# A two-layer decoder on one core: the RWKV-7 recurrence taken 16 heads at a time instead of 8

## The chip, the cores and the metric

One core of a Trainium2 chip. A core has a matrix engine (TensorE, PE in the profile, with its weight loads as PEld), VectorE (DVE), ScalarE (ACT), GpSimd (POOL) and SyncE (SP, which issues the DMAs here). The metric is the device time of one execution in microseconds; a kernel is described by the median of its runs.

## The reference, cut to what matters

The model has two layers on 272 tokens (16 meta tokens and 256 others) of width 2048, each a token mixer and a squared-ReLU MLP. The mixer of layer 0 is RWKV-7 with 32 heads of 64; that of layer 1 is gated linear attention and is not touched here. The part around the change is this:

```python
def step(S, inp):
    r_t, w_t, k_t, v_t, a_t, b_t = inp
    sa = jnp.einsum('bhvk,bhk->bhv', S, a_t)
    S = S * w_t[:, :, None, :] + sa[..., None] * b_t[:, :, None, :] + v_t[..., None] * k_t[:, :, None, :]
    y = jnp.einsum('bhvk,bhk->bhv', S, r_t)
    return S, y
_, y = lax.scan(step, S0, xs)
...
mu = jnp.mean(y, axis=-1, keepdims=True)
var = jnp.mean(jnp.square(y - mu), axis=-1, keepdims=True)
y = ((y - mu) * lax.rsqrt(var + RW_GN_EPS)).reshape(B, T, D) * ln_w + ln_b
out = ((y + bonus).astype(x.dtype) * g) @ w_o
```

Every head carries a 64x64 state S through all tokens. The kernel does not step by token: it takes chunks of 64 tokens (four of them and a last one of 16). Inside a chunk the dependence of a token on earlier ones is a triangular system, which is inverted; from chunk to chunk only S is passed.

## The kernel before, in words

All activations lie transposed: a tile of 128 features by 272 tokens, 16 such tiles (f = 0 to 15), each with two heads. Weights come as blocks of 128x1024 in float32; `wload` (L126) has one DMA into `raw` (3 buffers), ScalarE rounds to `hi` and VectorE takes the rest as `lo` (2 buffers each), and `mm3` (L140) makes a product of three matmuls of 272 columns.

The mixer has three stretches that matter.

**The k loop** (L468 to L517). For each f it makes the key projection (48 matmuls), reads the decay and the learning rate back from HBM, and writes two tiles, `bk` and `ar`, to HBM (L491, L494). Two small matmuls hang on it, at L481 and L496; the second needs `kn` from VectorE. At f = 3 the first group's tiles are read back by `load(0)` (L417); from f = 5 to 9 `scores` makes the group's products of keys and queries, one chunk a time; from f = 10 the inversion of group 0 runs, 9 steps in each f.

**The products.** The v projection (256 units), then the output projection (256 units) are cut into units of three matmuls. `R(n)` runs n units, `until(n)` runs units up to the n-th; they fill TensorE between the steps of the recurrence. Units 0 to 255 are v; the output projection follows, and what it needs is `split` from the normed tiles of four f each: units 256, 288, 384 and 448 are the first that need the next four.

**The recurrence** (L784 to L857). TensorE's order is written out by hand there (`manual_schedule`); the order of the other engines is the scheduler's, which takes program order as priority and puts weight loads ahead of the rest. Four groups of 8 heads are taken one after the other, and each goes through five chunks:

- `scores` (L423) makes a chunk's products; two VectorE multiplies with a mask write them into `AM`.
- `invert` (L439) is VectorE's: 8 transposes into `sysA` (2 more for the last chunk), 30 steps of two tensor ops each, 12 transposes back. It is written as a generator, and `some(inv, n)` puts n steps at a place in the order. `merge` (L539) then joins two inverted blocks of 32 into one of 64, by two rounds of 32x32 matmuls with ScalarE copies between.
- `centre` (L569) takes the values, for two chunks at once, `keys` (L582) transposes the keys.
- `inner`, `state`, `sides`, `solve`, `carry`, `learn`, `emit` (L590 to L657) are the chunk itself: `state` applies S from the last chunk, `sides` copies the right side negated, `solve` applies the inverse, `learn` makes the new S (ScalarE scales it in four pieces, L647), `emit` the output. Each works through its heads by small matmuls whose even and odd heads lie in different halves of the array.
- `norm` (L659) is the group norm and the gate of four f; it follows each group.

A chunk's step waits for the step before it, so units stand between: `GAPS` (L46) has their number ahead of `solve` and ahead of `learn`, for each group and chunk. `MARK` (L51) has the unit up to which units run before a group's inversion must be done.

In the order of TensorE, the scores of group g+1 lie in chunks 0 and 1 of group g, its inversion runs from there to `until(MARK[g])`, and then `merge(g+1)` follows:

```python
until(MARK[g])
some(inv, 99)
m = merge(g + 1)
next(m)
```

Of the kernel before, what the change touches and what calls it, by code (L numbers as in the profile page):

```python
# [1 line left out]

# [15 lines left out]
P = 128  # L18
# [27 lines left out]
GAPS = [[(4, 3), (4, 3), (8, 7), (8, 7), (6, 6)],  # L46
# [3 lines left out]

MARK = [162, 256, 366]  # L51
# [5 lines left out]
class Kern:  # L57
# [210 lines left out]
    def rwkv(self, done):  # L268
# [147 lines left out]
        def fetch(g, dst, src, a=0, b=576):  # L416
            nc.sync.dma_start(dst[g % 2][:, :, a:b], src[4 * g : 4 * g + 4, :, a:b].rearrange("f p n -> p f n"))  # L417

        def load(g):
            fetch(g, BKs, bkd)  # L420
            fetch(g, ARs, ard)

        def scores(g, c):  # L423
            BK, AR, AM, AMr = (b[g % 2] for b in (BKs, ARs, AMs, AMrs))
            n = C if c < NC4 else 32
            cs = slice(c * 128, c * 128 + 2 * n)

            pv = [self.ptr().rearrange("p (h m) -> p h m", h=4)[: 2 * n, :, : 2 * n] for _ in range(2)]
            for p in range(4):
                for q in range(2):  # L430
                    rows = slice(64 * q, 64 * q + 64)
                    nc.tensor.matmul(pv[q][:, p], BK[rows, p, cs], AR[rows, p, cs], start=True, stop=True)  # L432
            dst, mk = (AM[:, c], self.maskA) if c < NC4 else (AMr, self.maskR)
            for q in range(2):
                tt(dst[:, q::2], pv[q], mk.unsqueeze(1).to_broadcast([2 * n, 4, 2 * n]))
# [3 lines left out]
        def invert(g):  # L439
            AM, AMr = AMs[g % 2], AMrs[g % 2]  # L440
            X = sysA
            diag = lambda u: AM[64 + 32 * u : 96 + 32 * u, :, :, 32 * u : 32 * u + 32].rearrange("p c h t -> p t c h")
            part = [slice(8 * k, 8 * k + 8) for k in range(4)]
            nc.gpsimd.memset(X[64:96], 0.0)
# [4 lines left out]
            for k in part[:2]:  # L449
                nc.vector.transpose(X[96:128, k], AMr[32:64, :, k].rearrange("p h t -> p t h").unsqueeze(2)  # L450
                                    .to_broadcast([32, 8, 4, 8]))
                yield
            nc.gpsimd.memset(X.rearrange("p a b -> p (a b)")[:, ::33], 1.0)
            for s in range(1, 31):
                n, m = 31 - s, s
                w = self.t(lp, [P, 256], "upd", 1)[:, : n * m].rearrange("p (a b) -> p a b", a=n)
                tt(w, X[:, s + 1 :, s : s + 1].to_broadcast([P, n, m]), X[:, s : s + 1, :m].to_broadcast([P, n, m]))
                tt(X[:, s + 1 :, :m], X[:, s + 1 :, :m], w, ALU.add)
                yield
# [8 lines left out]
        for f in range(KT):  # L468
# [30 lines left out]
            if f == 0:  # L499
# [4 lines left out]
                BKs, ARs = ([self.t(lp, [P, 4, 576], n)] for n in ("BK0", "AR0"))  # L504
                AMs, AMrs = [self.t(lp, [P, NC4, 8, 128], "AM0")], [self.t(lp, [64, 8, 64], "AMr0")]
                sysA = self.t(lp, [P, 32, 32], "sysA")
                t11 = sysA.rearrange("p a b -> p (a b)")[64:96].rearrange("p (c h s) -> p c h s", c=NC4, h=8)
# [14 lines left out]
        BKs.append(self.t(kp, [P, 4, 576], "BK1"))  # L522
        ARs.append(self.t(kp, [P, 4, 576], "AR1"))
        AMs.append(self.t(kp, [P, NC4, 8, 128], "AM1"))
        AMrs.append(self.t(kp, [64, 8, 64], "AMr1"))
        sb = self.t(kp, [P, 4, HEAD], "S")
        half = lambda x: x[:, :256].rearrange("p (h v) -> p h v", h=4)
        uvs, ras, bkts, rys, pSs = {}, {}, {}, {}, {}

        def geom(g, c):  # L530
            full = c < NC4
            n = C if full else 32
            lo, up = slice(0, n), slice(n, 2 * n)


            return full, n, C if full else T - NC4 * C, (AMs[g % 2][:, c] if full else AMrs[g % 2]), lo, up, (up, lo)


        def merge(g):  # L539
            AM, AMr = AMs[g % 2], AMrs[g % 2]  # L540
            rg = self.t(kp, [P, 512], "rs", 2)[32:64].rearrange("p (t s) -> p t s", t=16)
            nc.vector.transpose(rg, sysA[96:128, 0:16])
            nc.vector.tensor_copy(AMr[32:64, :, 0:16].rearrange("p h t -> p t h"), rg[:, :, 0:8])
            qs = {}
            for c in (0, 2):

                pq = self.ptr()
                qs[c] = self.t(kp, [P, 512], "rs", 2) if c else self.t(kp, [P, 4, P], "bkt", 1).rearrange("p a b -> p (a b)")
                for h in range(8):
                    for i in range(2):  # L550
                        nc.tensor.matmul(pq[64 + 32 * i : 96 + 32 * i, 32 * h : 32 * h + 32], AM[64:96, c + i, h, 32:64],
                                         t11[:, c + i, h], start=True, stop=True)
                for i in range(2):
                    nc.scalar.copy(qs[c][96:128, 256 * i : 256 * i + 256], pq[64 + 32 * i : 96 + 32 * i, :256])
            yield
            for c in (0, 2):
# [557 lines left out]
```

## Time and profile before

| what | value |
|---|---|
| median of 3 runs | 2589.22 us (2586.8 to 2591.66) |
| the profiled execution | 2593.35 us |
| its span | 2591.6 us |
| PE busy | 2543.9 us (98%) |
| DVE busy | 1664.5 us (64%) |
| ACT busy | 1262.3 us (49%) |
| PE busy, 296 to 671 us of the span | 351.10 of 375.00 us |
| DVE busy there | 280.67 us |
| ACT busy there | 200.83 us |

The stretch from 296 to 671 us holds the units and the recurrence; the k loop lies ahead of it. A busy PE is not PE at its peak: matmuls are pipelined, and a record lasts longer than the time to the next one's start. In the timeline, the distance of starts is what a matmul costs. One float32 matmul of the recurrence stands as two records, while one of the units (rounded operands) stands as one. PEclk is the share of TensorE's clock that was granted.

### The profile page before, as it was taken

The numbers are of one execution on the slowest core, as the hardware profiler recorded it, in microseconds if no ns is written. First come the engines' busy times: TensorE is split into PE (matmuls) and PEld (weight loads), VectorE is DVE, ScalarE is ACT, GpSimd is POOL, SyncE is SP. The second block draws the span as 40 slices with busy tenths as digits, with TensorE's granted clock in tenths as the row PEclk, the third lists the DMA queues.
The fourth block names the chain that finished last, engine by engine and source line by source line (L and its number), as shares of the span: only waits on it lengthen the run. The fifth ranks groups of instructions, "written<-read, shape, count | busy, mean of one in ns | idle before, by whom it ended". The sixth has DMA issues, their size and how long they took to land.

```text
span 2591.6 us, 47101 instructions
## 1 busy us (share of the span) xinstructions
PE 2543.9 (98%) x19222; PEld 2351.8 (91%) x19222; DVE 1664.5 (64%) x2749; ACT 1262.3 (49%) x2055; POOL 11.4 (0%) x36
## 2 busy tenths in 40 slices
PE   9999999999999999999999999999999999999998
PEld 8898888888999999999999988998888888888887
DVE  8677977885655545445456676668666656656565
ACT  5475555546544334334334455445555435445444
POOL 0000000000000000000000000000000000000000
PEclk9999999999999999999999999999999999999999
DMA  5476733432455555545555544444555555555554
GB/s 202 169 246 236 231 133 112 133 112 98 163 176 174 179 174 177 179 172 179 176 174 179 173 153 147 147 154 171 187 188 188 189 189 189 187 187 187 188 189 160
DMA packets 137082, 450.14 MB, mean 174 GB/s; under 512 B 15760, under 2 KB 23696, under 8 KB 136864
## 3 DMA queue, kind: packets, MB, share of 16 engines
q1 hardware_dynamic: 136864, 447.12, 50.0%
q8 instruction: 151, 2.47, 0.4%
q14 instruction: 67, 0.55, 0.1%
HBM read 431.07 MB, written 15.99 MB: 173 GB/s over the span
## 4 chain that ended last, share of the span: by engine, by line
PE 89%; DVE 7%; ACT 1%; issue 1%; DMA 1%; DVEq 0%; POOL 0%; ACTq 0%; SPq 0%; POOLq 0%
PE pj L170 24%; PE pj L142 14%; PE pj L144 14%; PE pj L143 14%; PE pj L171 12%; DVE lo L137 2%; DVE sysA L270 1%; DVE upd L270 1%; PE pj L197 1%; PE pt L432 1%; PE pm L684 1%; DVE AM L465 1%; DVE sysA L447 1%; PE pt L949 1%; ACT hi L136 0%
## 5 line engine op out<-in xcount | busy, mean ns | idle before, releaser
L136 ACT CAST hi<-raw 128x1024 fp32r<-128x1024 f32 (+2 forms) x838 | 814.0, 979 | 1105.4 <-PE pj L143 589.6
L137 DVE TENSOR_TENSOR lo<-raw,hi 128x1024 fp32r<-128x1024 f32 (+2 forms) x838 | 946.5, 1136 | 576.0 <-ACT hi L136 567.8
L142 PE MATMUL pj<-x,hi 128*128 128x272 f32 x2272 | 674.1, 297 | 9.9 <-DVE hres L270 6.4
L144 PE MATMUL pj<-x,lo 128*128 128x272 f32 x2272 | 659.5, 290 | 6.4 <-DVE lo L137 6.2
L143 PE MATMUL pj<-x,hi 128*128 128x272 f32 x2272 | 658.6, 290 | 0.6 <-DVE x L270 0.6
L170 PE MATMUL pj<-x,hi 128*128 128x512 f32 x1664 | 585.8, 396 | 0.6 <-DVE x L868 0.6
L171 PE MATMUL pj<-x,lo 128*128 128x256 f32 x1664 | 466.7, 281 | 1.3 <-DVE lo L137 1.3
L142 PEld LDWEIGHTS pj<-x,hi 128*128 128x128 f32 x2272 | 430.6, 190 | 18.9 <-issue 6.3
L144 PEld LDWEIGHTS pj<-x,lo 128*128 128x128 f32 x2272 | 430.3, 189 | 9.3 <-DVE lo L137 8.2
L143 PEld LDWEIGHTS pj<-x,hi 128*128 128x128 f32 x2272 | 433.3, 191 | 3.3 <-DVE x L270 0.9
L170 PEld LDWEIGHTS pj<-x,hi 128*128 128x128 f32 x1664 | 312.5, 188 | 77.0 <-issue 2.9
L170 PE MATMUL pj<-h,hi 128*128 128x512 f32 x1024 | 358.5, 394 | 0.0
L171 PEld LDWEIGHTS pj<-x,lo 128*128 128x128 f32 x1664 | 313.3, 188 | 2.2 <-DVE lo L137 1.9
L142 PE MATMUL pj<-h,hi 128*128 128x272 f32 x1024 | 294.7, 288 | 0.0
L144 PE MATMUL pj<-h,lo 128*128 128x272 f32 x1024 | 293.9, 287 | 0.0
L143 PE MATMUL pj<-h,hi 128*128 128x272 f32 x1024 | 293.5, 287 | 0.0
L171 PE MATMUL pj<-h,lo 128*128 128x256 f32 x1024 | 288.5, 282 | 0.0
L170 PEld LDWEIGHTS pj<-h,hi 128*128 128x128 f32 x1024 | 192.4, 188 | 44.5
L143 PEld LDWEIGHTS pj<-h,hi 128*128 128x128 f32 x1024 | 193.7, 189 | 0.0
L171 PEld LDWEIGHTS pj<-h,lo 128*128 128x128 f32 x1024 | 193.5, 189 | 0.0
L142 PEld LDWEIGHTS pj<-h,hi 128*128 128x128 f32 x1024 | 192.6, 188 | 0.0
L144 PEld LDWEIGHTS pj<-h,lo 128*128 128x128 f32 x1024 | 192.1, 188 | 0.0
(247 smaller groups left out, 2104.5 us busy)
## 6 DMA issues: line engine op xcount, KB each, us to landing
raw<-mlp_w_d SPq DMA_DIRECT2D x512, 512.0 KB, 3.3
raw<-gla_in_d SPq DMA_DIRECT2D x98, 512.0 KB, 3.2
raw<-w_rkv_d SPq DMA_DIRECT2D x80, 512.0 KB, 3.6
raw<-gla_o_d SPq DMA_DIRECT2D x32, 512.0 KB, 3.2
raw<-rw_oQ_d SPq DMA_DIRECT2D x24, 512.0 KB, 3.3
raw<-w_r_d SPq DMA_DIRECT2D x16, 512.0 KB, 3.3
ard<-ar SPq DMA_DIRECT2D x16, 288.0 KB, 4.0
bkd<-bk SPq DMA_DIRECT2D x16, 288.0 KB, 4.0
```

Of the source, the lines that this page charges most:

```text
L136: nc.scalar.copy(hi[:, h], raw[:, h])
L137: nc.vector.tensor_tensor(out=lo[:, h], in0=raw[:, h], in1=hi[:, h].bitcast(F32), op=ALU.subtract)
L142: nc.tensor.matmul(out, hi[:, ws], xh, start=first, stop=False)
L143: nc.tensor.matmul(out, hi[:, ws], xl, start=False, stop=False)
L144: nc.tensor.matmul(out, lo[:, ws], xh, start=False, stop=last)
L170: nc.tensor.matmul(wide, hi[:, ws], x[kt][:, :, off : off + SEQ], start=kt == 0, stop=False)
L171: nc.tensor.matmul(ps[:, :SEQ], lo[:, ws], x[kt][:, 0, off : off + SEQ], start=False, stop=kt == nk - 1)
L197: nc.tensor.matmul(ps[:, :n], raw[:, j * P : (j + 1) * P], x(kt), start=kt == 0, stop=kt == 8 * len(srcs) - 1)
L270: tt = lambda o, a, b, op=ALU.mult: nc.vector.tensor_tensor(out=o, in0=a, in1=b, op=op)
L432: nc.tensor.matmul(pv[q][:, p], BK[rows, p, cs], AR[rows, p, cs], start=True, stop=True)
L447: nc.vector.transpose(X[32 * u : 32 * u + 32, k], diag(u)[:, k])
L465: nc.vector.transpose(diag(u)[:, k], X[32 * u : 32 * u + 32, k])
```

## The change

Two halves of 16 heads take the place of four groups of 8. A half's four chunks and the last one are inverted in two blocks: block 2g has chunks 0 and 1, block 2g+1 has chunks 2, 3 and the last. `scores`, `invert` and `merge` go by these blocks, and `b` or `c > 1` picks the buffer.

- In the k loop, `load(0)` comes at f = 7 and reads 256 columns of eight f; the scores of block 0 come at f = 10 to 13; the inversion starts after f = 13, 6 steps in each f.
- The products start with 10 units, then five times 16 units and a piece of block 1's scores, with 7 steps of inversion 0 each. Merge 0 comes at unit 120.
- `MARK` = 120, 176, 244, 326 are the units ahead of merges 0, 1, 2 and 3; merges 1 and 3 lie between chunks 1 and 2. The gaps are 4 or 5 units.
- The scores of block 2 lie in chunks 2 and 3 of the first half, and its inversion runs from chunk 3. The scores of block 3 come after the first `inner` of the second half.
- The norms of the first eight f lie before and around merge 2, those of the other eight at the end.
- `centre` takes one chunk of 16 heads: two matmuls side by side, each with 64 tokens. `solve` makes the even heads first, copies them, then the odd heads. `state` sets its products for the right side ahead of most of those for the output. `learn` scales S by one VectorE multiply instead of four ScalarE ops.
- A block that holds chunks 0 and 1 is inverted on 64 partitions, the other on 128; the ops have the same free size as before.

The core of the diff:

```diff
-GAPS = [[(4, 3), (4, 3), (8, 7), (8, 7), (6, 6)],
-        [(4, 3), (4, 3), (8, 7), (8, 7), (6, 6)],
-        [(3, 2), (3, 2), (8, 7), (8, 7), (6, 6)],
-        [(4, 4), (4, 4), (4, 4), (4, 4), (4, 4)]]
-MARK = [162, 256, 366]
+GAPS = [[(4, 4), (4, 4), (5, 4), (5, 4), (5, 5)],
+        [(4, 4), (4, 4), (5, 4), (5, 4), (5, 5)]]
+MARK = [120, 176, 244, 326]
...
-            if f == 3:
+            if f == 7:
                 load(0)
-            if 4 < f < 10:
-                scores(0, f - 5)
-            if f == 9:
+            if 9 < f < 14:
+                scores((f - 10) // 2, f % 2)
+            if f == 13:
                 inv = invert(0)
-            if f > 9:
-                for _ in range(9):
+            if f > 13:
+                for _ in range(6):
                     next(inv, None)
...
 def centre(g, c):
-            for p in range(4):
-                nc.tensor.matmul(pv[:w, p * P : (p + 1) * P], hres[:, 4 * g + p, c * C : c * C + w], self.cent,
-                                 start=True, stop=True)
+            for p in range(4):
+                for e in range(2):
+                    nc.tensor.matmul(pv[64 * e : 64 * e + nr, p * P : (p + 1) * P], hres[:, 8 * g + 4 * e + p, c * C : c * C + nr],
+                                     self.cent, start=True, stop=True)
...
 def state(g, c):
-            turns = [(p, q, i) for p in range(4) for q, i in ((0, 0), (1, 1), (1, 0), (0, 1))]
-            if not full:
-                turns.sort(key=lambda x: x[2])
+            pq = [(p, q) for p in range(8) for q in range(2)]
+            turns = [(*x, 0) for x in pq]
+            outs = [(p, 1 - q, 1) for p, q in pq]
+            if full:
+                for i in range(7):
+                    turns.insert(1 + 3 * i, outs.pop(0))
+            for p, q, i in turns + outs:
...
 def solve(g, c):
-            for h in range(8):
-                o = n * (1 - h % 2)
-                nc.tensor.matmul(pu[o : o + nu, h // 2], am[up, h, :nu], rs[up, h], start=True, stop=True)
             for q in range(2):
                 o = n * (1 - q)
+                for h in range(q, 16, 2):
+                    nc.tensor.matmul(pu[o : o + nu, h // 2], am[up, h, :nu], rs[up, h], start=True, stop=True)
                 nc.scalar.copy(uv[n : n + nu, q::2], pu[o : o + nu])
...
 def learn(g, c):
-            for p in range(4):
-                nc.scalar.mul(sb[:, p], pS[:, p], WC[:, 4 * g + p, c : c + 1])
+            tt(sb, pS, WC[:, 8 * g : 8 * g + 8, c : c + 1].to_broadcast([P, 8, HEAD]))
...
         load(1)
         ahead()
         with tc.manual_schedule(engines={mybir.EngineType.PE}):
-            until(52)
-            m = merge(0)
+            R(10)
+            for c, e in ((2, 0), (2, 1), (3, 0), (3, 1), (4, 0)):
+                some(inv, 7)
+                R(16)
+                scores(c, e)
+            for g in range(2):
+                last, quarter = nothing, 0
+                if g:
+                    last = norm(0)
+                    some(last, 1)
+                    for _ in range(4):
+                        R(3)
+                        some(last, 2)
+                    last = chain(last, norm(1))
+                until(MARK[2 * g])
+                some(inv, 99)
+                m = merge(2 * g)
+                next(m)
...
+                until(128 + 128 * g)
+                centre(g, 0)
...
+                inv = invert(2 * g + 1)
                 for c in range(5):
+                    if c == 2:
+                        until(MARK[2 * g + 1])
+                        some(inv, 99)
+                        m = merge(2 * g + 1)
...
                     if c:
                         state(g, c)
+                    if g == 0 and c in (2, 3):
+                        scores(c - 2, 0)
                     R(GAPS[g][c][0])
-                    some(inv, 9)
+                    some(inv, 11)
                     solve(g, c)
-                    if c in (1, 3):
+                    if c < 4:
                         centre(g, c + 1)
+                    if g == 0 and c in (2, 3):
+                        scores(c - 2, 1)
                     if c < 4:
                         carry(g, c)
                     R(GAPS[g][c][1])
+                    if g == 0 and c == 3:
+                        inv = invert(2)
+                    some(inv, 11)
...
+                    if g == 0 and c == 1:
+                        load(2)
+                    if g == 0 and c == 4:
+                        load(3)
+            for g in (2, 3):
+                for _ in norm(g):
+                    R(g)
```

More of the change, by code (lines that the diff above doesn't have):

```diff
@@ L1 @@
 from contextlib import ExitStack
+from itertools import chain
 import numpy as np
@@ L430, in scores, with load @@
+        def load(b):
+            fetch(b, BKs, bkd)
+            fetch(b, ARs, ard)
+        def scores(c, e):
+            BK, AR = BKs[c > 1], ARs[c > 1]
+            n, np = (C, 4) if c < NC4 else (32, 8)
+            o = 128 * (c % 2) if c < NC4 else 256
+            cs = slice(o, o + 2 * n)
+            pv = [self.ptr().rearrange("p (h m) -> p h m", h=np)[: 2 * n, :, : 2 * n] for _ in range(2)]
+            for p in range(np):
                 for q in range(2):
                     rows = slice(64 * q, 64 * q + 64)
-                    nc.tensor.matmul(pv[q][:, p], BK[rows, p, cs], AR[rows, p, cs], start=True, stop=True)
@@ L590, in inner @@
         def inner(g, c):
-            full, n, nr, am, lo, up, at = geom(g, c)
+            full, n, nr, am, lo, up, at = geom(c)
             uv = uvs[g, c]
-            ra = ras[g, c] = half(self.pu())
-            for h in range(8):
-                nc.tensor.matmul(ra[at[h % 2], h // 2], am[:n, h, :n], uv[:n, h], start=h < 2, stop=c == 0 and h > 5)
+            ra = ras[g, c] = bank(self.pu())
+            for h in range(16):
+                nc.tensor.matmul(ra[at[h % 2], h // 2], am[:n, h, :n], uv[:n, h], start=h < 2, stop=c == 0 and h > 13)
@@ L606, in state @@
         def state(g, c):
[L607 to L614 removed]
+            full, n, nr, am, lo, up, at = geom(c)
+            AR, ra = ARs[c > 1], ras[g, c]
+            o = 128 * (c % 2) if full else 256
```

237 lines of the change are left out of this document (101 added, 136 removed).

## The prediction

> **What bounds the kernel now.** I read the page first, then windows, the timeline of PE, the waits of PE and the groups of VectorE.
>
> ```profile
> span 2591.6 us, 47101 instructions
> PE 2543.9 (98%) x19222; PEld 2351.8 (91%) x19222; DVE 1664.5 (64%) x2749; ACT 1262.3 (49%) x2055; POOL 11.4 (0%) x36
> ```
>
> TensorE sets the end: a gain must take matmul time away or close holes in PE. The change touches the k loop and the recurrence, so I asked for windows: 210 to 230 us in the k loop, three that reach from the first to the last VectorE op of an inversion, and one between inversions. Behind the window stand its length and the busy time of PE, PEld, DVE, ACT and POOL, then PEclk.
>
> ```profile
> 210.00:230.00 20.00, 17.28 (x116) 15.70 (x115) 8.71 (x19) 7.09 (x14) 0.00 (x0) 0.74 0.64 239
> 350.85:396.45 45.60, 42.19 (x547) 38.09 (x545) 43.20 (x105) 21.78 (x55) 0.69 (x2) 1.00 0.38 135
> 432.85:478.75 45.90, 43.65 (x578) 40.06 (x579) 43.45 (x104) 22.98 (x58) 0.69 (x2) 0.96 0.37 134
> 510.15:561.95 51.80, 46.75 (x587) 43.24 (x586) 49.80 (x121) 23.52 (x55) 0.68 (x2) 1.00 0.27 94
> 400.00:432.00 32.00, 30.95 (x448) 27.04 (x446) 15.81 (x29) 20.00 (x47) 0.94 (x1) 1.00 0.35 110
> ```
>
> While an inversion runs, DVE is busy for 43.2 of 45.6 us, 95%, and PE idles for 3.4, 2.2 and 5.1 us, 10.7 in all. Between inversions DVE is half free. So the recurrence is bound by PE, with holes where VectorE is short. The second window, asked for the inversion's tile alone:
>
> ```profile
> 350.85:396.45 45.60, 0.00 (x0) 0.00 (x0) 33.22 (x83) 0.17 (x1) 1.00 0.38 135
> ```
>
> An inversion is 33.2 us of VectorE, and there are four of them before and after.
>
> **Small matmuls: minus 9.2 us.**
>
> ```profile
> 343.26 0.27 PE L620 MATMUL pu<-S,AR 64*64 64x64 f32 x1
> 343.27 0.27 PE L617 MATMUL pry<-AR,S 64*64 64x64 f32 x1
> 343.28 0.27 PE L620 MATMUL pu<-S,AR 64*64 64x64 f32 x1
> ...
> 343.37 0.22 PE L620 MATMUL pu<-S,AR 64*64 64x64 f32 x1
> ...
> 343.72 0.22 PE L620 MATMUL pu<-S,AR 64*64 64x64 f32 x1
> ...
> 343.89 1.16 PE L432 MATMUL pt<-AR,BK 64*128 64x128 f32 x16
> 344.98 0.39 PE L142 MATMUL pj<-x,hi 128*128 128x272 f32 x1
> 345.21 0.29 PE L143 MATMUL pj<-x,hi 128*128 128x272 f32 x1
> 345.33 0.29 PE L144 MATMUL pj<-x,lo 128*128 128x272 f32 x1
> ```
>
> `state` of 8 heads is 16 matmuls in 8 rounds of four records each. Rounds lie 0.058 us apart (343.37 to 343.72, six steps), yet the group takes from 343.26 to 343.89, 0.63 us: 0.16 beyond eight rounds, paid where a group begins and ends. Unit matmuls lie 0.125 apart, so a unit is 0.375 us; the first distance of a run is 0.23, and with its end I take 0.2 more for a run. Groups of double length halve their number: inner, solve and emit fall from 20 to 10 each, learn, state and keys from 16 to 8, and 54 x 0.16 is 8.6 us. The runs of units hardly change (71 to 67).
>
> ```profile
> 347.29 1.16 PE L574 MATMUL pm<-cst,hres 128*128 128x128 f32 x8
> 348.38 1.16 PE L432 MATMUL pt<-AR,BK 64*128 64x128 f32 x16
> 349.47 0.70 PE L639 MATMUL pu<-S,cst 128*128 128x256 f32 x2
> 349.82 0.48 PE L142 MATMUL pj<-x,hi 128*128 128x272 f32 x1
> ```
>
> `centre` took 1.09 us, twelve times (four of them for the last chunk). With two column halves side by side, its 16 records should take what the 16 paired ones of L432 take, 1.09, ten times: minus 2.2, of which I take 1.6. `carry`, 0.35 us, at most doubles and halves its number: 0. `state` gives up its rounds of four: 16 products for the right side need 16 rounds, as many as two groups had, and the outputs that find no partner cost up to ten rounds more, 0.6 us, six times; I take 1, between 0 and 3.5.
>
> `solve` is the open price. Its even and odd heads alternated between two column halves; now eight matmuls of one half stand ahead of eight of the other. Paired they cost 16 rounds, one behind another 32: 0.93 us more, ten times, 9.3. In the rows above each matmul stands as two records, and L617's first record starts ahead of L620's second: a matmul does pass earlier ones that use another quarter, three of them in a round of four. I take 0, since eight is not far from three, and keep 9.3 as the other end.
>
> The Trainium skill ("TensorE: Matmul & The Clock Gate", Part 3: Packing small matmuls) says that matmuls start and end strictly in program order. By it the sum would be 9.3 us higher. The alternating rows do not agree with it.
>
> **The k loop: minus 10.6 us.** Its timeline on PE, and two waits of PE from 170 to 320 us:
>
> ```profile
> 205.09 0.73 PE L481 MATMUL pm<-sq,cst 128*128 128x272 f32 x2
> ...
> 212.28 0.72 PE L481 MATMUL pm<-sq,cst 128*128 128x272 f32 x2
> 215.72 2.08 PE L432 MATMUL pt<-AR,BK 64*128 64x128 f32 x16 [2.72 <-DMA AR<-ard]
> ...
> 218.13 0.43 PE L143 MATMUL pj<-x,hi 128*128 128x272 f32 x1
> 218.35 0.43 PE L144 MATMUL pj<-x,lo 128*128 128x272 f32 x1
> ```
>
> ```profile
> PE pu L496 <- DVE kn L492: 3.4, 4, 1.4
> PE pt L551 <- DVE sysA L461: 1.5, 1, 1.5
> ```
>
> The first scores wait 2.7 us for the read-back of `AR`, and then a matmul takes 0.22 us instead of 0.125. PEclk is 0.74 over these 20 us: 5.2 us of clock are missing, so some 10.4 us ran at half; the slowdown from 0.125 to 0.22 loses 0.43 of that, 4.5 us. An f takes 7.2 us (205.09 to 212.28). With the load at f = 7 and the scores at f = 10, three f lie between where two lay, so `AR` comes 4 us early instead of 3 us late: minus 2.7 and 4.5. The inversion took 33 us of VectorE out of f = 10 to 15; 12 of its 52 steps stay, so I let 2.8 of the 3.4 us at L496 go. One small piece of scores (0.6 us) leaves the loop. Bounds: 0, if VectorE and the read-back stay late, to minus 13, if every delay of those f goes.
>
> **VectorE's windows: plus 13.3 us.**
>
> ```profile
> L137 DVE TENSOR_TENSOR lo<-raw,hi 128x512 fp32r<-128x512 f32 x100 | 64.4, 686 | 12.3 <-ACT hi L136 11.6
> L270 DVE TENSOR_TENSOR AM<-pt,cst 128x512 f32<-128x512 f32 x24 | 15.5, 686 | 23.5 <-PE pt L432 23.5
> L270 DVE TENSOR_TENSOR hres<-pj,hres 128x272 f32<-128x272 f32 x22 | 9.6, 438 | 23.9 <-PE pj L144 23.1 <-DMA hres<-hT_d 0.8
> L679 DVE SCALAR_TENSOR_TENSOR ysq<-hres,vecs,ysq 128x272 f32<-128x272 f32 x16 | 8.0, 498 | 6.9 <-ACT ysq L675 6.9
> L684 PE MATMUL pm<-gs,g 128*128 128x272 f32 x60 | 16.8, 403 | 3.2 <-ACT uv L580 2.1 <-ACT bkt L587 1.0
> ```
>
> A unit asks VectorE for 0.16 us of `lo` (two ops of 0.64 busy in 8 units) and its product for 0.44, once in 16 units (v) or 4 (output). A norm of four f asks it for 5.7 (three ops like L679's and L270's in each f) and PE for 4.2 (16.8 for 16 f). The new scaling of S, 512 columns out of PSUM as at `AM`, asks for 0.69. From an inversion's start to its merge there were 80, 71 and 90 units; now there are 52, 46 and 51: units 124 to 176, 198 to 244 and 275 to 326. PE time at hand against demand on VectorE, with a chunk's six groups at 1.09, 6.5 us, and 2.1 more for state and carry:
> - inversion 0: units 45.0, scores 5.4, runs 1.2: 51.6. Demand 24.3 (38 of 52 steps) + 19.2 + 3.1 + 6.9 (scores) + 5 (the k loop's tail, two thirds of an f): 58.5. Short by 6.9.
> - inversion 1: units 19.5, the first centre, keys and inner 3.3, chunks 0 and 1 15.2, runs 1.6: 39.6. Demand 33.2 + 8.3 + 1.3 + 1.4: 44.2. Short by 4.6.
> - inversion 2: units 17.3, the rest of chunk 3 3.3, chunk 4 4.6, norm 4.2, runs 1.6: 31.0. Demand 32.0 + 7.4 + 1.3 + 5.7 + 0.7: 47.1. Short by 16.1.
> - inversion 3: units 19.1, chunks 15.1, runs 1.2: 35.4. Demand 33.2 + 8.2 + 5.7 + 1.8 (split) + 1.4: 50.3. Short by 14.9.
>
> That is 42.5 us. The same reckoning gives 4.3, 6.3 and 9, 19.6 in all, for the windows of before, where PE idles for 10.7: 0.55 of it. I take 0.6, as long stalls bring half clock: 25.5. Before it was 10.7 and the 1.5 at L551. The rest is 13.3, between 11 and 30.
>
> The chain from chunk to chunk I cost at 0:
>
> ```profile
> L603 ACT ACTIVATE rs<-pu 64x256 f32<-64x256 f32 x32 | 12.1, 377 | 0.9
> L580 ACT COPY uv<-pm 64x512 f32<-64x512 f32 x16 | 9.3, 580 | 2.3 <-PE pm L574 2.2
> ```
>
> Its copies grow from 0.38 to 0.58 us; four units, 1.5 us, and the outputs of `state` cover the two ahead of `solve`, which now needs one to begin. The scaling of S moves into VectorE's queue, perhaps behind several inversion ops; inner, emit and keys, 3.3 us, cover it, and where VectorE is short PE waits at the merge in any case. Without that cover it costs about 1 us a chunk.
>
> **The load of block 1: 0, up to plus 15.**
>
> ```profile
> 310.69 0.33 SPq L494 DMA_DIRECT2D ard<-ar  x1
> ...
> 318.04 5.37 SPq L130 DMA_DIRECT2D raw<-w_rkv_d  x2
> 323.46 0.43 SPq L417 DMA_DIRECT2D AR<-ard  x1
> ```
>
> ```profile
> DMA to landing us min/median/max: 3.2/7.5/9.7
> ```
>
> `AR1` was issued 12.8 us after the last `ard`, behind two weight loads in SP's queue, and such a load lands after 7.5 us. Its first use moves from unit 67 to unit 26, 9.8 us into the units. If the last `ard` goes out some 5 us into them PE waits up to 15 us, and everything behind in the hand-written order with it. VectorE uses that wait for inversion 0, whose 6.9 us are then not missing at merge 0; so I take 0 beyond the windows' sum.
>
> **Sum.** -9.2 - 10.6 + 13.3 = -6.5 us. The profiled execution is 2593.35 us (span 2591.6), 4.1 above the median of the runs; the difference goes on the median, 2589.2 - 6.5 = 2583. A measurement of this kernel tells about 0.2%, 5.2 us, from no change.
>
> **Rivals.**
> - *Solve's halves run one behind the other*: 9.3, and 2.5 for `state`; half of it lies in windows where PE waits anyway: +6, 2589. For it: no row shows passing over more than three matmuls. The skill's rule above would give the same.
> - *The load of block 1 decides* (slower): where `AR1` lands more than 17 us after the first unit, its wait is longer than VectorE's shortage hides. At 24 us it is 14 of wait and 4.5 of half clock, less 4.5 hidden: +14, 2597. For it: SP's order above. Against: the last `ard` may go out earlier.
> - *VectorE's shortage in full*: 30.3 in place of 13.3, +17, 2600. Against: the windows of before show half of their reckoning.
> - *The read-back is late at f = 10 too* (that part does not do what it says): +7.2, 2590.
> - *No more shortage than before*, since VectorE works ahead: -13, 2570.
>
> **Chances.** Forecast 0.42 (its own range 2577 to 2589), solve 0.20, load 0.15, full shortage 0.08, read-back 0.08, no shortage 0.07. Faster by over 0.2%: 0.7 of the forecast, a quarter of solve, and the last, 0.41. Slower: most of load and full shortage, and a little of the others, 0.26. Same: 0.33. The range, 2567 to 2602, holds all these places but the far ends of the last three.
>
> **What would show it.** No wait of L432 and no half clock in the k loop. `solve` in groups of 32 records of about 1.1 us (1.95 if not paired). PE idle for 6 to 9 us ahead of merges 2 and 3, with VectorE at 95%. A wait for `AR` at unit 26 under 10 us. The forecast is wrong if PE's idle time from the first unit to the last passes 45 us, or if PE waits for S.

## The result and the profile after

The changed kernel takes 2623.6 us (median of 4 runs, 2622.2 to 2625.8) against 2588.5 for the kernel before beside it: 1.0135 times, 95% interval 1.0117 to 1.0153. It is some 35 us slower, 41 above the forecast and above its range. The profiled execution is 2624.24 us, 30.9 more than that of before, which was itself some 4 us above the median of its runs. The page of the changed kernel:

```profile
span 2622.0 us, 47088 instructions
PE 2555.0 (97%) x19274; PEld 2364.8 (90%) x19274; DVE 1667.9 (64%) x2745; ACT 1239.7 (47%) x1941; POOL 9.3 (0%) x32
```

Windows of the changed kernel: two in the k loop, ten microseconds early in the products, and the stretch from the first unit to the end of the last one. Behind the window stand its length, the busy time of PE, PEld, DVE, ACT and POOL, PEclk, DMA share and GB/s.

```profile
210.00:230.00 20.00, 20.00 (x146) 18.90 (x145) 16.80 (x47) 14.53 (x28) 0.00 (x0) 1.00 0.81 266
230.00:250.00 20.00, 19.35 (x160) 18.12 (x159) 10.97 (x21) 10.68 (x19) 0.00 (x0) 1.00 0.85 293
300.00:310.00 10.00, 0.00 (x0) 0.00 (x0) 9.36 (x22) 0.00 (x0) 0.00 (x0) 0.72 0.98 327
293.05:698.72 405.67, 362.13 (x4366) 331.57 (x4364) 289.08 (x650) 174.47 (x356) 4.26 (x7) 0.93 0.35 115
```

The same stretch of the kernel before:

```profile
296.56:668.15 371.59, 347.69 (x4302) 315.45 (x4300) 278.89 (x631) 198.76 (x474) 5.40 (x10) 0.98 0.37 126
```

The k loop gave 3.5 us in these two executions (the first unit starts at 293.05, not 296.56), and the stretch lost 34.1. Of those, 19.6 are idle time of PE (43.5 against 23.9) and 14.4 are busy time, with a mean clock of 0.93 in place of 0.98. In the window from 300 to 310 PE does nothing at all. Its waits over the stretch:

```profile
PE pt L436 <- DMA AR<-ard: 12.6, 1, 12.6
PE pt L557 <- DVE sysA L466: 11.0, 2, 8.2
PE pu L641 <- ACT uv L642: 6.7, 10, 0.7
PE pj L141 <- DVE hres L269: 4.1, 8, 1.4
PE pm L692 <- DVE hres L693: 2.8, 2, 1.7
PE pu L631 <- DVE S L269: 2.1, 1, 2.1
```

The columns are the total, how often, and the longest. L436 is the scores, L557 the merge, L641 `solve`, L631 `state`. In the kernel before, the first three came to 1.5 us, all at the merge.

PE's timeline at the first and the third of these rows:

```profile
299.19 0.29 PE L143 MATMUL pj<-x,lo 128*128 128x272 f32 x1
312.06 1.23 PE L436 MATMUL pt<-AR,BK 64*128 64x128 f32 x8 [12.58 <-DMA AR<-ard]
...
373.88 1.14 PE L641 MATMUL pu<-rs,AM 64*64 64x64 f32 x16
375.69 1.14 PE L641 MATMUL pu<-rs,AM 64*64 64x64 f32 x16 [0.67 <-ACT uv L642]
376.76 0.66 PE L580 MATMUL pm<-cst,hres 128*64 128x128 f32 x8
```

A solve of 16 heads takes from 373.88 to 376.76, 2.88 us: 0.92 for the even heads, 0.89 until the odd ones start, 1.07 for these. A solve of 8 in the kernel before:

```profile
346.68 0.68 PE L630 MATMUL pu<-rs,AM 64*64 64x64 f32 x16
347.29 1.16 PE L574 MATMUL pm<-cst,hres 128*128 128x128 f32 x8
```

Two such groups took 2 x 0.61. The eight matmuls of a half do not run beside the other eight, and the second half also waits for ScalarE's copy of the first. And in SyncE's queue:

```profile
295.72 0.42 SPq L499 DMA_DIRECT2D ard<-ar  x1
297.73 0.33 SPq L129 DMA_DIRECT2D raw<-w_rkv_d  x1
298.87 0.37 SPq L419 DMA_DIRECT2D BK<-bkd  x1
301.87 0.33 SPq L129 DMA_DIRECT2D raw<-w_rkv_d  x1
302.30 0.38 SPq L419 DMA_DIRECT2D AR<-ard  x1
```

`AR1` is issued 6.6 us after the last `ard` and the scores start 9.8 us after that, while the DMA engines are 98% busy.

### The profile page after: what moved, and what is told of

Read it like the earlier page. It is cut to its first block, busy times and chain, and to the rows that moved or that the text cites. A ratio compares the mean times of both kernels' runs of the same rounds, so it can differ in the third digit from the quotient of the medians.

```text
span 2622.0 us, 47088 instructions
## 1 busy us (share of the span) xinstructions
PE 2555.0 (97%) x19274; PEld 2364.8 (90%) x19274; DVE 1667.9 (64%) x2745; ACT 1239.7 (47%) x1941; POOL 9.3 (0%) x32
## 4 chain that ended last, share of the span: by engine, by line
PE 78%; DVE 2%; ACT 1%; DMA 0%; issue 0%; DVEq 0%
PE pj L169 24%; PE pj L141 13%; PE pj L143 13%; PE pj L142 13%; PE pj L170 12%; DVE lo L136 1%; PE pt L970 1%; PE pu L641 0%; PE pu L979 0%; PE pm L692 0%; PE pt L959 0%; PE pu L981 0%; PE pry L681 0%; PE pm L580 0%; PE pm L916 0%; PE pu L980 0%
```

## The experiments

The theory after this reading: (A) `solve`'s order, (B) the late load of block 1 and (C) VectorE's shortage make the stretch longer, 17, 13 and the rest. The rival: VectorE's shortage alone decides, and the others lie beside it. Then there is the k loop, which gave 3.5 of 10.6 us (D, E). The table has all runs; "stretch" runs from the first unit to the end of the last one in the profiled execution, and the ratio is to the kernel before, with its interval. "Both" is the changed kernel with the edits of `solve_alternates` and `scores_later`.

| kernel | first unit at | stretch | PE busy in it | PEclk | ratio |
|---|---|---|---|---|---|
| before | 296.56 | 371.59 | 347.69 | 0.98 | 1 |
| after | 293.05 | 405.67 | 362.13 | 0.93 | 1.0135 (1.0117 to 1.0153) |
| solve_alternates | 293.57 | 388.07 | 344.34 | 0.94 | 1.0067 (1.0044 to 1.0089) |
| solve_copies_last | 296.98 | 400.50 | 358.76 | 0.92 | 1.0093 (1.0060 to 1.0126) |
| scores_later | 292.55 | 396.68 | 359.75 | 0.94 | 1.0117 (1.0077 to 1.0157) |
| both | 295.61 | 382.12 | 346.14 | 0.95 | 1.0037 (1.0017 to 1.0056) |
| both_no_elimination | 295.30 | 350.25 | 335.70 | 0.98 | 0.9930 (0.9903 to 0.9957) |
| before_no_elimination | 295.91 | 352.33 | 340.26 | 0.99 | 0.9934 (0.9917 to 0.9950) |
| both_S_on_scalar | 293.98 | 376.14 | 343.07 | 0.95 | 1.0038 (1.0019 to 1.0056) |
| both_solve_by_two | 295.34 | 380.99 | 344.08 | 0.96 | 1.0048 (1.0024 to 1.0072) |
| both_solve_by_four | 293.34 | 382.49 | 346.30 | 0.96 | 1.0046 (1.0022 to 1.0070) |
| before_scores_f_later | 294.76 | 372.29 | 345.46 | 0.98 | 1.0008 (0.9990 to 1.0026) |
| both_ca_other_queue | 319.23 | 384.88 | 347.84 | 0.94 | 1.0138 (1.0100 to 1.0175) |
| before_ca_other_queue | 315.48 | 375.70 | 350.24 | 0.97 | 1.0081 (1.0047 to 1.0114) |
| both_readback_other_queue | 294.80 | 385.18 | 348.11 | 0.94 | 1.0068 (1.0043 to 1.0094) |
| before_readback_other_queue | 298.58 | 373.68 | 348.70 | 0.98 | 1.0022 (1.0003 to 1.0042) |
| after_readback_other_queue | 299.78 | 404.60 | 360.49 | 0.92 | 1.0138 (1.0123 to 1.0153) |
| both_no_readback | 291.05 | 382.13 | 345.24 | 0.95 | 1.0048 (0.9990 to 1.0106) |
| before_no_readback | 292.20 | 372.24 | 348.12 | 0.98 | 1.0003 (0.9977 to 1.0028) |
| best_of_all | 297.89 | 377.45 | 341.52 | 0.96 | 1.0050 (1.0035 to 1.0065) |

Where only the k loop was edited, the stretch of "both" came out at 382.1 to 385.2 and that of before at 371.6 to 375.7: such a stretch repeats within some 4 us, so differences of 6 or more are read from it. The first unit repeats no better: eight kernels have the changed k loop as it is (after, the two of `solve`, scores_later, both, both_S_on_scalar, by two, by four), and theirs starts between 292.55 and 296.98, 294.3 on average.

### solve: order and copies

Alternating heads again:

```diff
-            for q in range(2):
-                o = n * (1 - q)
-                for h in range(q, 16, 2):
-                    nc.tensor.matmul(pu[o : o + nu, h // 2], am[up, h, :nu], rs[up, h], start=True, stop=True)
-                nc.scalar.copy(uv[n : n + nu, q::2], pu[o : o + nu])
+            for h in range(16):
+                o = n * (1 - h % 2)
+                nc.tensor.matmul(pu[o : o + nu, h // 2], am[up, h, :nu], rs[up, h], start=True, stop=True)
+            for q in range(2):
+                o = n * (1 - q)
+                nc.scalar.copy(uv[n : n + nu, q::2], pu[o : o + nu])
```

> The changed kernel with one edit: solve's 16 heads alternate between the two column halves again, and both copies stand behind all of them. Theory A (solve's order cost the time: in the changed kernel a solve takes 2.88 us, two halves of 0.93 to 1.07 one behind the other and 0.89 between them, against 2 x 0.61 before, ten times): solve is one group of about 1.1 us and the time falls by about 16 us, from 2623.6 to 2607 (2603 to 2612, as some of it lies where VectorE is short). Rival (VectorE's shortage decides, and solve lies beside it): the waits ahead of the merges grow by what solve gives back, and the time stays within 2617 to 2624.

One solve of it on PE:

```profile
372.93 1.15 PE L640 MATMUL pu<-rs,AM 64*64 64x64 f32 x32
374.01 1.09 PE L580 MATMUL pm<-cst,hres 128*64 128x128 f32 x16
```

1.08 us, and the stretch is 17.6 shorter; the ratio falls by 0.0068, which is 17.6 us too. Theory A holds, and nothing of it was taken back by VectorE's waits.

The halves one behind the other, but both copies behind them:

```diff
-                nc.scalar.copy(uv[n : n + nu, q::2], pu[o : o + nu])
+            for q in range(2):
+                o = n * (1 - q)
+                nc.scalar.copy(uv[n : n + nu, q::2], pu[o : o + nu])
```

> The changed kernel with solve's two halves still one behind the other, but with both copies behind both halves. If the 0.89 us between the halves is a wait for the first half's copy and nothing else, solve becomes one group of 32 records of about 1.95 us without a gap, and the time falls by about 9, to 2615; what is left against the kernel whose heads alternate is the order alone, 0.8 to 0.93 a solve, 8 to 9 us. Rival (the copies come later now, and inner, learn and emit wait for them instead): the gap moves behind solve and the time stays at 2621 to 2624.

```profile
378.06 1.90 PE L641 MATMUL pu<-rs,AM 64*64 64x64 f32 x32
379.89 1.09 PE L580 MATMUL pm<-cst,hres 128*64 128x128 f32 x16
```

1.83 us without a gap. The stretch falls by 5.2, the ratio by 0.0042 (11 us); its interval is wide, so the wait for the copy is worth 5 to 11, and the order the rest of the 17.6.

How many matmuls may stand between two that run side by side? `both` with runs of two and of four of one half (`for h in [0, 2, 1, 3, 4, 6, 5, 7, ...]` and `[0, 2, 4, 6, 1, 3, 5, 7, ...]`):

> The changed kernel with block 1's scores later, and solve's heads in runs of two of one column half (two even, two odd, ...) ahead of both copies. Theory (a matmul passes some earlier ones of another quarter, as in the rounds of state, but not eight): a solve takes the 1.1 us of alternating heads, or up to 1.2. Rival (a matmul passes none; only direct neighbours run side by side): only every second pair meets, about 1.5 us.

```profile
378.78 1.20 PE L640 MATMUL pu<-rs,AM 64*64 64x64 f32 x32
379.90 1.09 PE L580 MATMUL pm<-cst,hres 128*64 128x128 f32 x16
```

> As the run by two, but in runs of four (four even, four odd, twice). If three can be passed and four cannot, a solve takes 1.5 to 1.7 us; if four can be passed, 1.1 to 1.2; if only direct neighbours meet, about 1.75.

```profile
377.67 1.54 PE L640 MATMUL pu<-rs,AM 64*64 64x64 f32 x32
379.14 1.09 PE L580 MATMUL pm<-cst,hres 128*64 128x128 f32 x16
```

So the price of the order is a ladder: 1.08 us with runs of one, 1.12 of two, 1.47 of four, 1.83 of eight. A matmul passes one or two of the other half at almost no cost, four in part, and eight hardly. The starts of the 32 records show the same. With runs of eight they lie 0.058 us apart (378.065 to 378.813 for the first 13), and only around the change of half do three pairs start within 0.006 us of each other; with runs of two they start in pairs, within 0.015 us, throughout.

### The load of block 1

```diff
             R(10)
-            for c, e in ((2, 0), (2, 1), (3, 0), (3, 1), (4, 0)):
-                some(inv, 7)
-                R(16)
-                scores(c, e)
+            for _ in range(3):
+                some(inv, 7)
+                R(16)
+            for c, e in ((2, 0), (2, 1), (3, 0), (3, 1), (4, 0)):
+                scores(c, e)
+                if (c, e) in ((2, 0), (3, 0)):
+                    some(inv, 7)
+                R(8 if c < 4 else 0)
```

> The changed kernel with the first scores of block 1 at unit 58 and then every 8 units, in place of unit 26 and every 16; the inversion's steps stay at their units. Theory B (the late load decides: PE waits 12.9 us for AR and runs at half clock behind it): no wait there, the time falls by 13 to 16, to 2608 to 2611. Rival, the prediction's (VectorE used that wait, and its shortage shows at merge 0 instead): PE waits at merge 0 for 7 to 12 us, and the time is 2616 to 2623.

> The changed kernel with both edits, heads alternating in solve and block 1's scores later. If the two causes are apart, the falls add up: 2591 to 2596. If VectorE's shortage takes their place, the waits ahead of the merges grow and the time is 2602 or more.

The wait for `AR` falls from 12.6 to 2.8 and 3.3 us, and PE does not wait at merge 0. Alone the stretch is 9.0 shorter, behind `solve_alternates` 6.0: less than the 13 to 16 expected, and the two add up to 23.6 of 26.6. The ratio of "both", 1.0037, is some 2599 us: between the two expectations. Waits for `lo` (2.8 us at a time) come in its place, so VectorE does take a part back, though not where the rival had it. The median of `scores_later` itself says little: its four runs spread from 2615 to 2634.

### VectorE's shortage

In `invert`, for both kernels (the transposes, scores and merges stay; the elimination is what is left out):

```diff
             for s in range(1, 31):
+                yield
+                continue
```

> The changed kernel with heads alternating in solve and block 1's scores later, and with the 30 elimination steps left out of every inversion (its transposes, the scores and the merges stay), so that VectorE has some 25 us less to do in each of four inversions. Theory C (what is left against the kernel before is VectorE's shortage): the waits of 9.0 and 5.0 us ahead of merges 2 and 3, the 2.4 for S and the 3.6 at the output products go, and the stretch from the first unit of the products to the layer's end falls from 382 to 355 to 362 us, as long as the kernel before has it without its elimination, or up to 9 shorter. Rival (TensorE's own work in the recurrence has grown): the stretch stays 5 to 10 longer than in the kernel before without elimination.

> The kernel before with the 30 elimination steps left out of every inversion, the counterpart of the run above. Theory C: it gains less than the changed order does, 10 to 13 us of 372 between the first unit and the layer's end. Rival: both gain alike, and the difference of 10 between them stays.

The stretch of "both", with and without the elimination, and that of before without it:

```profile
295.61:677.73 382.12, 346.14 (x4367) 319.00 (x4365) 288.17 (x650) 174.37 (x356) 4.25 (x7) 0.95 0.38 122
```

```profile
295.30:645.55 350.25, 335.70 (x4366) 309.79 (x4364) 216.06 (x414) 174.84 (x356) 4.26 (x7) 0.98 0.41 132
```

```profile
295.91:648.24 352.33, 340.26 (x4298) 311.18 (x4296) 207.18 (x403) 197.69 (x471) 5.40 (x10) 0.99 0.40 130
```

With 72 us less for VectorE the changed order is 31.9 us faster, the order before 19.3; the remaining difference of 10.5 turns into 2.1 the other way. So VectorE's shortage costs the changed order 12.6 us more (10.6 by the ratios: 27.7 against 17.1), and TensorE's own work in it is not longer: the 2.1 lies within the 4 us by which a stretch repeats. Both kernels gain more than was expected (10 to 13 us for the order before); the difference is the one that theory C asks for. PE's waits in "both" (the first fence) and without the elimination show where:

```profile
PE pt L557 <- DVE sysA L466: 13.5, 2, 8.7
PE pj L141 <- DVE hres L269: 6.9, 7, 4.4
PE pj L143 <- DVE lo L136: 4.1, 2, 2.8
...
PE pm L693 <- DVE hres L694: 2.8, 2, 1.7
PE pu L631 <- DVE S L269: 2.4, 2, 2.1
```

```profile
PE pu L633 <- DVE S L269: 3.8, 2, 2.1
...
PE pj L141 <- DVE hres L269: 2.5, 6, 1.2
PE pj L143 <- DVE lo L136: 1.8, 2, 1.1
PE pm L695 <- DVE hres L696: 1.3, 2, 1.2
```

The waits at merges 2 and 3 go, and most of those for the output products. The wait for S stays: the op that scales S stands in VectorE's queue behind the inversion's first transposes (in the changed kernel they end at 448.09 and it starts at 448.13), and these are not left out. With ScalarE scaling S again (`nc.scalar.mul(sb[:, p], pS[:, p], WC[:, 8 * g + p, c : c + 1])` for eight `p`):

> The changed kernel with heads alternating in solve and block 1's scores later, and S scaled by ScalarE again, in eight pieces a chunk in place of one op of VectorE. If S waits behind VectorE's queue and that queue is what is short: PE's wait of 2.4 us for S goes, VectorE has 5.5 us less to do, and the time falls by 4 to 6. Rival (eight pieces of ScalarE, some 0.2 us each, are a longer path to state than one op): PE waits 0.5 to 1 us for S in each of eight chunks, and the time is 4 to 8 higher.

PE no longer waits for S, and the stretch is 6.0 shorter than that of "both"; the ratios, 1.0038 and 1.0037, show no difference. The trace agrees with the theory, the times leave it open; the rival (slower) is out.

### The k loop

The first scores and the first inversion of the kernel before one f later (it leaves out the last seven of inversion 0's 52 steps, for which no f is left):

```diff
-            if 4 < f < 10:
-                scores(0, f - 5)
-            if f == 9:
+            if 5 < f < 11:
+                scores(0, f - 6)
+            if f == 10:
                 inv = invert(0)
-            if f > 9:
+            if f > 10:
```

> The kernel before with its first scores and its first inversion one f later in the k loop (f = 6 to 10 in place of 5 to 9). The prediction's step for the k loop: the wait of 2.7 us for AR and the half clock behind it (4.5) go, and the time falls by about 7, to 0.997 of before. Rival (VectorE's late f and merge 0 take it back, as the changed kernel's f = 11 to 15 did): 0.999 to 1.001.

```profile
216.22 1.16 PE L432 MATMUL pt<-AR,BK 64*128 64x128 f32 x16 [1.17 <-DMA AR<-ard]
```

The wait is 1.2 in place of 2.7 us, f = 7 takes 9.2 us in place of 18.6, and the first unit starts only 1.8 earlier: the later f and merge 0 (PE idles for 6.4 us ahead of it, 1.5 before) take it back, and the ratio, 1.0008, is the rival's. So the wait and the clock behind it, which the prediction had priced, were not what the k loop was waiting for.

In the changed kernel VectorE has a hole of the same size as before, from 230 to 250 (11.0 of 20 us, against 8.7). The first idea was that `ca` stands behind the read-back in SyncE's queue:

```diff
-            nc.sync.dma_start(ca.rearrange("p a t -> p (a t)"), cad[f])
+            nc.gpsimd.dma_start(ca.rearrange("p a t -> p (a t)"), cad[f])
```

> The changed kernel with heads alternating in solve and block 1's scores later, and the k loop's loads of ca issued by GpSimd in place of SyncE. Theory D (the k loop hardly gained, because the read-back of block 0 stands ahead of two loads of ca in SyncE's queue: VectorE is busy for 11 of 20 us there and PE pays for it in f = 11 to 15): the hole of VectorE goes, f = 11 to 15 fall from 8 to 12 us each towards 8, and the first unit starts at 287 to 290 in place of 293 to 296; the time falls by 5 to 7. Rival (the transfers of the read-back themselves fill the DMA engines, whatever queue ca stands in): the hole stays and the time is the same within 3.

> The kernel before with the loads of ca issued by GpSimd in place of SyncE. Theory D: the same queue makes the wait at its f = 7 longer (VectorE 8.7 of 20 us there); f = 7 falls from 18.6 us to 10 to 12 (the wait for AR stays) and the time falls by 4 to 7, to 0.9975 to 0.9985 of before. Rival: the transfers are the limit, same time.

Both miss: the first unit starts 19 to 24 us later. ScalarE's waits from 205 to 285 us in the first of them:

```profile
ACT iW L481 <- DMA ca<-cad: 33.7, 7, 6.5
```

Against 3.0 in "both": from GpSimd's queue `ca` was issued 8 to 12 us apart, and ScalarE waited for it seven times in a row. The pair says what a late `ca` costs, and nothing of the hole. So the read-backs were moved instead (`nc.gpsimd.dma_start` in `fetch`):

> The changed kernel with heads alternating in solve and block 1's scores later, and the read-backs (BK, AR) issued by GpSimd in place of SyncE; ca stays in SyncE's queue. Theory D (in the k loop ca stands behind the read-back, W and iW wait for it, and VectorE has a hole): ca is issued every 7 to 8 us throughout, the hole of VectorE (11.0 to 12.6 of 20 us busy) goes, and the first unit starts 4 to 8 us earlier, at 287 to 291. Rival (the 2 MB of the read-back fill the DMA engines and ca and the weights come late all the same): first unit at 293 to 296 as now.

> The kernel before with the read-backs issued by GpSimd in place of SyncE. Theory D: ca is on time, and if GpSimd issues AR as early as SyncE did the wait of 2.7 us for AR and the half clock behind it go as well: f = 7 falls from 18.6 us to 8 to 12 and the time falls by 5 to 8, to 0.997 to 0.998 of before. Rival (the transfers limit): 0.9995 to 1.001.

> The changed kernel with nothing changed but the queue of the read-backs. If AR of block 1 is late because of its place in SyncE's queue (issued 6.6 us behind the last ard, behind BK and a weight load), PE's wait at unit 26 falls from 12.9 us to 4 to 7, and the time falls by 5 to 8 there and by what the k loop gains. If it is late because the last ard is late and the transfer takes 7 to 10 us, the wait stays at 10 to 13.

No gain in any of the three. The first scores of block 1 in the third of them wait as long as ever:

```profile
319.26 2.08 PE L436 MATMUL pt<-AR,BK 64*128 64x128 f32 x16 [13.05 <-DMA AR<-ard]
```

There `AR1` was issued 4.8 us after the last `ard`, not 6.6, and the scores started 16.4 us after it, as against 16.3: the earlier issue gained nothing, and the place in SyncE's queue is not shown to be the cause of the wait at unit 26. Of theory D the first half holds. In "both" no `ca` is issued between 219.08 and 242.53, with the read-backs on GpSimd's queue one goes out every 6 to 11 us, and VectorE is busy for 36.4 us from 205 to 250 in place of 32.3. Its price does not hold: the first unit starts only 0.8 us earlier, within the spread. Last, the first read-back left out altogether:

```diff
-            if f == 7:
-                load(0)
...
                 nc.gpsimd.memset(sysA, 0.0)
+                nc.gpsimd.memset(BKs[0], 0.0)
+                nc.gpsimd.memset(ARs[0], 0.0)
```

> The changed kernel with heads alternating in solve and block 1's scores later, and with the read-back of block 0 left out: BK0 and AR0 are filled with zeros by GpSimd at f = 0, so the scores of block 0 are computed from zeros. Theory E (the read-back's 2 MB, which take the DMA engines to 0.85 to 0.95 and hold up ca and the weights, make VectorE's hole, and PE pays for it in f = 11 to 15): VectorE stays above 17 of 20 us from 225 to 245, and the first unit starts 5 to 8 us earlier than with the read-back, at 287 to 290 in place of 295. Rival (the scores' own work on PE, VectorE and ScalarE makes f = 11 to 15 slow): the first unit starts at 293 to 296 all the same.

> The kernel before with the read-back of the first four f left out in the same way (BK0 and AR0 hold zeros). Theory E: the wait for AR, the half clock and VectorE's hole at f = 7 (18.6 us) go together, f = 7 takes 8 to 9, and the first unit starts at 287 to 290 in place of 296.6. Rival: f = 8 to 15 get slower by what f = 7 gains, since VectorE's work is the limit, and the first unit starts at 293 to 296.

The window from 225 to 245 us in "both", with the read-back on GpSimd's queue, and without it:

```profile
225.00:245.00 20.00, 18.36 (x143) 17.31 (x143) 12.57 (x26) 10.73 (x18) 0.00 (x0) 1.00 0.92 297
```

```profile
225.00:245.00 20.00, 16.88 (x128) 15.55 (x127) 14.22 (x38) 12.39 (x23) 1.90 (x2) 1.00 0.95 345
```

```profile
225.00:245.00 20.00, 19.55 (x149) 18.26 (x148) 16.81 (x46) 14.38 (x27) 0.00 (x0) 1.00 0.82 268
```

VectorE's busy time goes from 12.6 over 14.2 to 16.8 of 20 us, and from 205 to 285 us from 62.7 over 63.8 to 67.4: over the whole stretch the queue is worth little, the transfers more. But the read-back costs the k loop only 4.6 us in the changed kernel (295.61 to 291.05; 3.3 against the average of 294.3) and 4.4 before (296.56 to 292.20): about as much in one as in the other, by one execution of each. It falls between theory E's 5 to 8 and the rival's 0 to 3. The ratios, 1.0048 and 1.0003, show no gain; their intervals are too wide for 4 us. What remains lies where the scores and the inversion run: without any read-back f = 11 to 15 take 9.2 to 9.6 us each in the changed order, f = 6 to 10 before. Which of their parts makes an f 2 us longer was not taken apart.

### The best that was found

> The changed kernel with five edits: heads alternating in solve, block 1's scores later, read-backs issued by GpSimd, S scaled by ScalarE, and state's products in rounds of four again. Theory: 2602 of the first two edits, less 3 to 6 for S, 4 to 8 for the k loop and 2 for state: 2586 to 2593, as fast as the kernel before. Rival (VectorE's shortage at merges 2 and 3 takes the gains of the k loop back): 2595 to 2600.

1.0050 (1.0035 to 1.0065), some 2602 us: slower than the theory's range, and just above the rival's, which the interval still touches. Merge 2 alone waits 8.2 us there, as the rival has it. But the first unit starts at 297.89, so the gain of the k loop that both counted on did not come; the stretch is 4.7 us shorter than that of "both". No version of the changed order beat the kernel before, and no edit of the kernel before that does all of its work beat it; "both" comes closest, 0.4% behind.

## Why the prediction was wrong, point by point

| term | forecast | measured | from |
|---|---|---|---|
| small matmuls, heads alternating | -9.2 | -6.4 | PE, start to start less its idle time, in the two runs without elimination |
| the order of `solve` | 0 | +17.6 | after against solve_alternates |
| k loop | -10.6 | -3.5 | first unit, after against before |
| VectorE's windows | +13.3 | +12.6 | 31.9 less 19.3 |
| load of block 1 | 0 | +6.0 | solve_alternates against both |
| scores among the units (one small piece more) | 0 | +1.9 | as in the first row |
| sum | -6.5 | +28.2 | 30.9 between the profiled executions; 2.7 has no term |

Without the elimination PE idles 2.5 us longer in the changed order (14.6 against 12.1); that may be most of what has no term.

- **The step that failed is `solve`'s: "I take 0, since eight is not far from three."** Its upper end, 9.3, was sized well (the ladder gives 0.75 a solve, 7.5 in all, at full clock), but the ladder rises between two and eight, and the rows that the prediction quoted reached to three only. It also missed that a copy which now stands between the halves makes the second half wait, 0.67 us in each of ten solves. And the rival's discount, half of it hidden where PE waits anyway, did not hold: all 17.6 came out in the time. The load of block 1, set at 0, and the k loop, of which 3.5 of 10.6 came, helped to turn the sign of the forecast.
- The Trainium skill ("TensorE: Matmul & The Clock Gate", Part 3: Packing small matmuls) says that matmuls start and end strictly in program order. An estimate by that rule, record by record, is some 1.5 us for runs of two (25 steps of 0.058 and the end) and 1.9 for runs of eight. The 1.12 measured does not agree with it, and the measurement decides; 1.83 for runs of eight nearly agrees.
- **The load of block 1** was the rival that ends on the other side, and its mechanism is what the trace shows: 12.6 us of wait where 14 was reckoned. The forecast's reason for 0, that VectorE uses the wait for inversion 0, is half right: merge 0 has no wait, and taking the load's wait away brought 6 to 9 us, not 13.
- **The k loop** lost its wait for `AR` and its half clock, as forecast (PEclk 1.00 from 210 to 250), and still gained only a third: 3.5 us, or 2.3 by the average of the eight kernels. What failed there is pricing the wait that PE showed: behind it lay a hole in VectorE that the read-back makes in either order, at about 4 us in each, and later f grow when an earlier one shrinks. What f = 7 to 15 take beyond 7.2 us each sums to 17.4 us before; f = 11 to 15 take 13.1 beyond it after. Why an f with scores or inversion takes 2 us more stays open.
- **VectorE's windows** were right in the difference, 12.6 for 13.3, partly by luck. The elimination costs 31.9 us in the changed order and 19.3 before, where the sum had 25.5 and 12.2: both are off by about 7. Merges 0 and 1, with a shortage of 6.9 and 4.6 in the reckoning, have no wait even in "both". Merges 2 and 3 waited 8.2 and 2.8 us (8.7 and 4.7 in "both") where 6 to 9 was forecast for each.
- **Small matmuls** were right in direction: inner 20 x 0.61 to 10 x 1.07 (-1.6), emit -1.4, learn -1.2, keys -1.5, solve -1.0, carry -1.0. But `centre` gave 0.5 and not 1.6, and `state` took 1.8 more where the sum had 0.3 less (-1.3 for its eight groups and +1). Of that, 0.8 is one group at half clock (2.83 us for 2.05), behind the wait for S.
- **The chain** was not quite 0: PE waited 2.1 us for S once, behind an inversion's transposes on VectorE, which the prediction had named as a sign against it. Its other sign, more than 45 us of idle time, did not come: PE idled for 43.5.

## What to carry to other kernels

Order small matmuls so that partners in different parts of the array are neighbours or one apart, and don't put a reader of half a result between the halves that write it. A wait on the bounding engine is worth what is late behind it: before pricing it, look whether another engine has a hole at the same place. And a due time fixed by hand against the units, as the scores at unit 26, has to be checked against the landing of its data, not only its issue.

## What the runs showed of the hardware

- Eight pairs of 64 x 64 float32 matmuls on two column halves take 1.08, 1.12, 1.47 or 1.83 us as one, two, four or eight of a half stand in a row.
- In `solve` of the changed kernel the second half's first matmul started 0.89 us after the first half's last step, released by ScalarE's copy, though it writes the other 64 partitions of the tile. The Trainium skill ("PSUM — Partial Sum Buffer", PSUM bank collisions raise a hardware error) lets two engines use different quadrants of one bank at the same time. By that this wait is one that the program sets; no run here tried the halves in two tiles.
- Two read-backs of 1.25 MB issued within 3.4 us left the DMA engines 98% busy at 327 GB/s, and the scores that wait for the second started 9.8 us after its issue from SyncE's queue; issued from GpSimd's, 0.9 us behind the first, they started 11.6 us after.
